# Score units in one slot less of each pair, and one gate portion ahead of its first transposes

## The chip, the cores and the metric

One core of a Trainium2 chip runs the whole kernel. The metric is the device time of one execution in microseconds (us); lower is better. Matmuls and transposes run on TensorE (PE), elementwise work on VectorE (DVE) and ScalarE (ACT), some helpers on GpSimd (POOL), and transfers are issued by SyncE (SP) and POOL.

## The reference

A decoder block on 1024 tokens of width 1024. What bears on the change is the attention part: 8 query heads (two per pair of heads, four heads per key group), three attention branches per head, and a gate per branch.

```python
s = einsum(q, k_cmp) * scale;  p_cmp = masked_softmax(s, pos_c <= t)        # 63 compressed keys
s_sel = einsum(qb, k_sel) * scale;  p_sel = masked_softmax(s_sel, kpos <= qpos)  # causal, all blocks
s_win = einsum(qb, k_win) * scale;  p_win = masked_softmax(s_win, wmask)    # window of 512
o = g[0] * o_cmp + g[1] * o_sel + g[2] * o_win
x = x + (sigmoid(ga) * (o @ w_branch_attn) + sigmoid(gb) * b) @ w_out       # ga, gb: columns of h @ w_in
```

## The kernel before

The stages are: input projections, a pooling branch, the attention stage, the output projections, and an MLP. The attention stage lies between about 336 and 694 us of the trace, and the change touches it alone.

**Pairs.** The stage walks over 32 pairs (L718): query tile i from 0 to 7, and in each the four head pairs hp from 0 to 3. For a pair there is a part A and a part B. Iteration n of the loop at L736 writes part A of pair n between the steps of part B of pair n-1.

**Part A** (`units_a`, L662) is four score units, in this order: selected keys of head 0 (`unit_sel`), window of head 0 (`unit_win`), selected keys of head 1, window of head 1. A unit writes its scores with PE into a tile `psS` (L578, L579), adds masks with PE (L584), takes the row maximum on DVE (L595) and the exponential on ACT (L596). From pair 12 on there are two `psS` tiles, so a unit needs the tile of the unit two before it. The fourth unit also ends the pair's softmax: it makes the factors `cc` (L650 to L652), scales the rows `pS` on DVE (L657, L658) and `pW` on ACT (L659). Odd hp add a fifth entry, `nxt`, which splits the next 512 columns of queries (`split_q`, L564 to L571).

**Part B** (`units_b`, L670) has a list of steps. A slot transposes one group of probability blocks into `psT` on PE (`tr`, L686) and splits it into `ph` on ACT (L689) and `pl` on DVE (L690). The products with the values (`pv`, L697) follow one slot later and have no slot of their own. A last slot without a transposition ends the list. So `nslot` is the number of groups plus one: 3, 4, 5, 6, 7, 7, 8, 8 for the pairs of i = 0 to 7.

**Where the units go.** At slot k the loop writes entries of part A until their count reaches ceil(k * na / nslot), with na = 4, or 5 for odd hp; then `finish_units` writes the masks and the softmax; then comes the slot's transposition.

**Gate portions.** `ga_terms` (L546) holds 128 portions of three matmuls each into `psG`, which compute the merge gate `ga`, in eight blocks of 16; the weights of the last block are loaded only after an earlier pair's output is written (`after=`, L550). `advance` (L723) writes as many portions as the part B done so far has earned: 20 at first, and then in proportion to the pairs' weights. In the kernel before it is called after the transposition of every slot.

The text of the loop is a list in order of rank and not yet the order on the engines. The tile layer draws up each engine's order when the kernel is built, from this rank and from what it reckons to be ready, so a piece of later rank can stand in front.

Of the kernel before, what the change touches and what calls it, by code (L numbers as in the profile page):

```python
# [49 lines left out]
def build(tc, a, out, dbg=None):  # L50
# [13 lines left out]
    def pool(stack, name, bufs=1, space=None, side=None):  # L64
        kw = dict(name=name, bufs=bufs, reuse_waits="tile")
        if space is DRAM:
            kw.pop("reuse_waits")
        if space is not None:
            kw["space"] = space
        if side is not None:  # L70
            kw["side"] = side
        return stack.enter_context(tc.tile_pool(**kw))
# [362 lines left out]
    def load_q(i, g):  # L435
        qi = qp.tile([P, HALF], F32, name="qi", bufs=2)
        nc.sync.dma_start(qi, qd[i][:, g * HALF:(g + 1) * HALF])
        return qi
# [93 lines left out]
    with ExitStack() as st:  # L532
# [31 lines left out]
        def split_q(qi):  # L564
            ps = psT.tile([P, HALF], F32, name="psT").rearrange("p (h n) -> p h n", h=4)
            for h in range(4):
                nc.tensor.transpose(ps[:, h], qi[:, h * P:(h + 1) * P], ident)
            qh = wk.tile([P, 4, P], F32R, name="qh", bufs=2)
            ql = wk.tile([P, 4, P], F32R, name="ql", bufs=2)
            nc.scalar.copy(qh, ps)  # L570
            nc.vector.tensor_tensor(ql, ps, f(qh), op=SUB)  # L571
            return qh, ql
# [9 lines left out]
        def finish_units():  # L582
            for ps, m, last, joint in masks_due:
                nc.tensor.matmul(ps, lhsT=identb, rhs=m, start=False, stop=last, skip_group_check=joint)  # L584
            for fn in softmax_due:
                fn()
            masks_due.clear()
            softmax_due.clear()
# [73 lines left out]
        def units_a(i, hp, q):  # L662
            w0 = max(0, i - WT)
            u = dict(i=i, hp=hp, g=hp // 2, w0=w0, nw=(i + 1 - w0) * P, pS=[], pW=[],
                     q=[(q[0][:, 2 * (hp % 2) + e], q[1][:, 2 * (hp % 2) + e]) for e in range(2)])
            for n in ("nm", "sm", "cc"):
                u[n] = wk.tile([P, 2, 3], F32, name=n, bufs=3)
            return u, [lambda e=e, fn=fn: fn(u, e) for e in range(2) for fn in (unit_sel, unit_win)]
# [54 lines left out]
        def advance(w):  # L723
            nonlocal done, given, ending
            done += w
            if len(bseq) and n >= len(pairs) - 1:
                ending += 0.4 * LAST / nslot
            while given < nterm and given < FIRST + (nterm - FIRST - LAST) * done / total + ending:
                next(fill, None)
                given += 1  # L730
# [4 lines left out]
        bseq, bw = [], 0  # L735
        for n in range(len(pairs) + 1):  # L736
            aseq = []
            if n < len(pairs):
                i, hp = pairs[n]
                if n == 12:  # L740
                    sctx.close()
                    psS = pool(sctx, "psS2", bufs=2, space=PSUM)
                u, aseq = units_a(i, hp, q)
                if hp % 2:
                    def nxt(j=2 * i + hp // 2 + 1):
                        nonlocal q, qnext
                        if j < 2 * NT:
                            q = split_q(qnext)
                            if j + 1 < 2 * NT:
                                qnext = load_q((j + 1) // 2, (j + 1) % 2)  # L750
                    aseq.append(nxt)
            na, nslot = len(aseq), max(1, sum(o for _, o in bseq))
            ia = k = 0
            for fn, slot in bseq or [(None, True)]:
                if slot:
                    k += 1
                    while ia < na and ia * nslot < k * na:
                        aseq[ia]()
                        ia += 1
                    finish_units()  # L760
                if fn is not None:
                    fn()
                if slot:
                    advance(bw / nslot)
            assert ia == na
            if n >= 2 and len(wsum) < 32 and summed < 27 * done / total:
                i, hp = pairs[n - 2]
                made[:] = [oT[0:1, hp, i * P:i * P + 4]]
                next(sums, None)
                summed += 1  # L770
            if n < len(pairs):
                bseq, bw = units_b(u), weight[n]
# [317 lines left out]
```

## Time and profile before

| | us |
|---|---|
| median of 3 runs (1469.38 to 1476.09) | 1470.88 |
| profiled execution, its own time | 1470.37 |
| its span | 1468.3 |
| PE busy | 1424.3 (97%) |
| DVE busy | 1008.9 (69%) |
| ACT busy | 756.4 (52%) |

The profile gives one execution. The span is from its first to its last instruction, 2.1 us less than the execution's time. A row of a timeline has the start in us, the duration in us, the engine, the line of the kernel, the operation, the tile written and the tiles read, the size, how many equal instructions it stands for, and in brackets the idle time of the engine just ahead of it with what ended it.

### The profile page before, as it was taken

To read this page: it belongs to the slowest core of one execution; us is meant where nothing else is said; L and a number is where in the kernel's file an instruction comes from. 1 tells how busy PE (TensorE), PEld (TensorE's weight loads), DVE (VectorE), ACT (ScalarE), POOL (GpSimd) and SP (SyncE) were. 2 spreads that over 40 slices of the span, in tenths; PEclk is the share of its full clock that TensorE was granted. 3 is DMA by queue.
4 is the path that set the end of the run, shared out by engine and by line. 5 is a ranking of instruction groups with operands and counts; after the bars stand their busy time and mean duration, and the time that the engine had idled before them with its cause. 6 is when DMAs were issued, how large, how long until landed. Compare 5 with 4: busy or idle time off the path is not lost.

```text
span 1468.3 us, 20380 instructions
## 1 busy us (share of the span) xinstructions
PE 1424.3 (97%) x7187; PEld 1177.9 (80%) x7187; DVE 1008.9 (69%) x1953; ACT 756.4 (52%) x1551; POOL 144.8 (10%) x207
## 2 busy tenths in 40 slices
PE   9989999999999999988999999999999999999996
PEld 7877888887778888776888888888888888888885
DVE  4793551114888888886758567667897386669996
ACT  4553231124888877776435363674344454764451
POOL 0006433222111211100000000000000000000000
PEclk9999999999999999999999999999999999999998
DMA  8334388886877777732845533333333223333323
GB/s 312 91 113 135 107 203 205 200 213 164 189 191 180 183 193 188 185 79 72 257 146 178 154 92 98 95 95 99 93 96 99 94 93 95 101 99 94 96 84 115
DMA packets 129109, 204.62 MB, mean 139 GB/s; under 512 B 9840, under 2 KB 60784, under 8 KB 128496
## 3 DMA queue, kind: packets, MB, share of 16 engines
q1 hardware_dynamic: 110800, 135.96, 29.9%
q0 software_dynamic: 17920, 67.11, 20.0%
q8 instruction: 56, 0.92, 0.2%
q14 instruction: 45, 0.37, 0.1%
q10 hardware_dynamic: 288, 0.27, 0.1%
HBM read 186.52 MB, written 83.89 MB: 184 GB/s over the span
## 4 chain that ended last, share of the span: by engine, by line
PE 89%; DVE 6%; ACT 3%; DMA 1%; issue 1%; SPq 0%; DVEq 0%; ACTq 0%
PE psm L78 17%; PE psm L77 17%; PE psm L79 17%; PE psF L78 5%; PE psF L79 5%; PE psF L77 5%; PE oacc L697 5%; PE psT L686 4%; PE psS L578 2%; PE psG L77 2%; PE psS L579 2%; PE psG L78 2%; PE psG L79 2%; PE acc L77 1%; PE acc L78 1%; PE acc L79 1%
## 5 line engine op out<-in xcount | busy, mean ns | idle before, releaser
L77 PE MATMUL psm<-mv,whi 128*128 128x512 f32 x896 | 350.6, 391 | 0.0
L78 PE MATMUL psm<-mv,whi 128*128 128x512 f32 x896 | 350.6, 391 | 0.0
L79 PE MATMUL psm<-mv,wlo 128*128 128x512 f32 x896 | 350.4, 391 | 0.0
L906 ACT CAST whi<-wraw 128x512 fp32r<-128x512 f32 x224 | 138.9, 620 | 257.3 <-PE psm L78 192.6
L82 DVE TENSOR_TENSOR wlo<-wraw,whi 128x512 fp32r<-128x512 f32 x289 | 197.8, 688 | 89.7 <-ACT whi L906 69.9
L78 PEld LDWEIGHTS psm<-mv,whi 128*128 128x128 f32 x896 | 168.3, 188 | 36.8
L77 PEld LDWEIGHTS psm<-mv,whi 128*128 128x128 f32 x896 | 168.3, 188 | 36.7
L79 PEld LDWEIGHTS psm<-mv,wlo 128*128 128x128 f32 x896 | 168.3, 188 | 36.7
L181 ACT CAST whi<-wraw 128x512 fp32r<-128x512 f32 x113 | 69.8, 621 | 125.4 <-PE psF L78 59.2
L690 DVE TENSOR_TENSOR pl<-psT,ph 128x512 fp32r<-128x512 f32 (+1 forms) x160 | 102.3, 648 | 31.3 <-ACT ph L689 29.6
L689 ACT CAST ph<-psT 128x512 fp32r<-128x512 f32 (+1 forms) x160 | 87.7, 556 | 47.9 <-PE psT L686 47.1
L595 DVE TENSOR_REDUCE nm<-psS 128x1 f32<-128x64 f32 (+8 forms) x192 | 100.2, 540 | 15.4 <-PE psS L584 10.1
L82 POOL TENSOR_TENSOR wlo<-wraw,whi 128x512 fp32r<-128x512 f32 x48 | 68.0, 1469 | 90.4 <-ACT whi L181 60.0
L77 PE MATMUL psF<-xh,whi 128*128 128x512 f32 x192 | 74.8, 390 | 0.0
L79 PE MATMUL psF<-xh,wlo 128*128 128x512 f32 x192 | 74.8, 390 | 0.0
L78 PE MATMUL psF<-xl,whi 128*128 128x512 f32 x192 | 74.7, 389 | 0.0
L596 ACT ACTIVATE pS<-psS,nm 128x64 f32<-128x64 f32 (+8 forms) x128 | 68.1, 534 | 8.7 <-DVE nm L595 8.0
L697 PE MATMUL oacc<-ph,vst 128*128 128x256 f32 x264 | 63.8, 320 | 4.1 <-ACT ph L689 2.7
L886 ACT CAST mv<-mt 128x512 fp32r<-128x512 f32 x96 | 59.0, 617 | 16.3 <-DVE mt L884 11.8
L82 DVE TENSOR_TENSOR mv<-mt,mv 128x512 fp32r<-128x512 f32 x96 | 65.1, 685 | 1.1 <-ACT mv L886 0.6
L686 PE MATMUL psT<-cf,pS 128*128 128x128 f32 x352 | 60.5, 277 | 4.5 <-DVE pS L657 4.2
L697 PE MATMUL oacc<-pl,vst 128*128 128x256 f32 x264 | 57.1, 295 | 3.1 <-DVE pl L690 3.0
(257 smaller groups left out, 2850.8 us busy)
## 6 DMA issues: line engine op xcount, KB each, us to landing
wraw<-wsw_ff SPq DMA_DIRECT2D x128, 256.0 KB
wraw<-in_w_ff SPq DMA_DIRECT2D x96, 256.0 KB
wsw_ff<-in_w_ff POOLq DMA_DIRECT2D x16, 1024.0 KB, 9.0
wsw_ff<-wsw_ff POOLq DMA_DIRECT2D x16, 1024.0 KB, 9.2
wraw<-in_w_in SPq DMA_DIRECT2D x48, 256.0 KB
wraw<-in_w_out SPq DMA_DIRECT2D x32, 256.0 KB
xt<-in_x SPq DMA_DIRECT2D x8, 512.0 KB
qd<-q SPq DMA_DIRECT2D x16, 256.0 KB
```

What stands on the lines that cost most here:

```text
L77: nc.tensor.matmul(ps, lhsT=sh, rhs=mh, start=first and i == 0, stop=False, skip_group_check=more)
L78: nc.tensor.matmul(ps, lhsT=sh, rhs=ml, start=False, stop=False, skip_group_check=more)
L79: nc.tensor.matmul(ps, lhsT=sl, rhs=mh, start=False, stop=last and i == n - 1, skip_group_check=more)
L82: eng.tensor_tensor(lo, src, f(hi), op=SUB)
L181: nc.scalar.copy(h, v)
L595: nc.vector.tensor_reduce(nm, v, axis=AX.X if flat else AX.XY, op=MAX, negate=True)
L596: nc.scalar.activation(p if flat else p.rearrange("p (a n) -> p a n", a=2), v, AF.Exp, bias=nm, accum_out=sm)
L686: nc.tensor.transpose(ps[:, j, e], src[e][:, c0:c0 + P], ident)
L689: nc.scalar.copy(ph[:, :n], ps[:, :n])
L690: nc.vector.tensor_tensor(pl[:, :n], ps[:, :n], f(ph[:, :n]), op=SUB)
L697: nc.tensor.matmul(o, lhsT=v, rhs=part[:, j], start=gi == 0 and j == 0 and part is ph, stop=2 * gi + j == nb - 1 and part is pl)
L906: nc.scalar.copy(hi, raw)
```

## The change

The entries of part A are spread over `nslot - 1` slots and not over `nslot`: at slot k their count reaches ceil(k * na / (nslot - 1)), so that all of them stand ahead of the last transposition. And in the first slot of a pair `advance` is called ahead of the transposition, in place of behind it. The number of portions that each call earns stays the same.

```diff
                 if slot:
                     k += 1
-                    while ia < na and ia * nslot < k * na:
+
+                    while ia < na and ia * max(1, nslot - 1) < k * na:
                         aseq[ia]()
                         ia += 1
                     finish_units()
+                    if k == 1:
+                        advance(bw / nslot)
                 if fn is not None:
                     fn()
-                if slot:
+                if slot and k > 1:
                     advance(bw / nslot)
```

## Rows read from the trace of the kernel before

**Rows 1.** The page: busy time of each engine.

```profile
PE 1424.3 (97%) x7187; PEld 1177.9 (80%) x7187; DVE 1008.9 (69%) x1953; ACT 756.4 (52%) x1551; POOL 144.8 (10%) x207
```

**Rows 2.** Busy time of each engine in the attention stage, by stretches.

```profile
core 0: us, PE busy (x) PEld busy (x) DVE busy (x) ACT busy (x) POOL busy (x), PEclk, DMA share, GB/s
336.00:430.00 94.00, 86.73 (x549) 69.97 (x549) 71.39 (x225) 68.74 (x228) 18.28 (x19) 1.00 0.72 171
430.00:606.00 176.00, 175.38 (x1217) 149.19 (x1216) 147.73 (x322) 138.66 (x330) 28.76 (x33) 1.00 0.78 194
606.00:673.00 67.00, 56.70 (x398) 46.50 (x398) 56.02 (x108) 50.93 (x110) 6.58 (x7) 1.00 0.44 99
673.00:694.00 21.00, 20.88 (x128) 17.56 (x126) 12.37 (x27) 10.28 (x21) 0.37 (x1) 1.00 0.20 63
```

**Rows 3.** The same stretches, instructions of the gate tile psG alone (PE, PEld, DVE).

```profile
336.00:430.00 94.00, 40.85 (x144) 25.31 (x144) 3.80 (x6) 1.00 0.72 171
430.00:606.00 176.00, 58.65 (x186) 31.13 (x186) 5.12 (x8) 1.00 0.78 194
606.00:673.00 67.00, 1.63 (x6) 1.05 (x6) 0.68 (x1) 1.00 0.44 99
```

**Rows 4.** Waits of PE, 606 to 673 us: total us, times, longest us.

```profile
PE psS L578 <- ACT pS L596: 2.7, 3, 1.3
PE oacc L697 <- ACT ph L689: 2.0, 4, 1.0
```

**Rows 5.** Timeline of PE in that stretch: five of the rows with a wait.

```profile
619.60 0.50 PE L578 MATMUL psS<-kds,qh 128*128 128x512 f32 x1 [1.42 <-ACT qh L570]
...
635.60 0.50 PE L578 MATMUL psS<-kds,qh 128*128 128x512 f32 x1 [0.75 <-ACT pS L596]
...
637.71 0.88 PE L686 MATMUL psT<-cf,pS 128*128 128x128 f32 x6 [0.39 <-DVE pS L657]
...
639.66 0.50 PE L697 MATMUL oacc<-pl,vst 128*128 128x256 f32 x2 [0.22 <-DVE pl L690]
...
663.86 0.50 PE L578 MATMUL psS<-kds,qh 128*128 128x512 f32 x1 [1.34 <-ACT pS L596]
```

**Rows 6.** Timeline of DVE between pair 28's last score unit and its first transposes.

```profile
630.84 0.82 DVE L595 TENSOR_REDUCE nm<-psS 128x1 f32<-128x640 f32 x1 [0.15 <-PE psS L584]
...
633.09 1.23 DVE L595 TENSOR_REDUCE nm<-psS 128x1 f32<-128x1024 f32 x1 [0.24 <-PE psS L584]
634.23 0.16 DVE L650 TENSOR_SCALAR cc<-sm 128x6 f32<-128x6 f32 x1
...
636.09 0.74 DVE L657 TENSOR_SCALAR pS<-pS,cc 128x1024 f32<-128x1024 f32 x1
```

**Rows 7.** Timeline of PE: one slot with no score unit and no gate.

```profile
640.00 0.60 PE L686 MATMUL psT<-cf,pS 128*128 128x128 f32 x4
...
640.91 0.60 PE L686 MATMUL psT<-cf,pS 128*128 128x128 f32 x4
```

**Rows 8.** Timeline of PE ahead of pair 18's first transposes.

```profile
504.62 0.47 PE L77 MATMUL psG<-xh,whi 128*128 128x512 f32 x1
...
506.97 0.40 PE L77 MATMUL psG<-xh,whi 128*128 128x512 f32 x1
...
507.66 0.40 PE L77 MATMUL psG<-xh,whi 128*128 128x512 f32 x1
...
508.05 0.44 PE L686 MATMUL psT<-cf,pS 128*128 128x128 f32 x2
```

**Rows 9.** Waits of PE, 336 to 430 us.

```profile
PE psT L686 <- DVE pS L657: 2.9, 4, 0.8
PE oacc L697 <- DVE pl L690: 1.4, 2, 1.1
```

**Rows 10.** Two early stretches, all engines: PE idle, then running.

```profile
82.00:84.00 2.00, 0.00 (x0) 0.00 (x0) 2.00 (x9) 0.44 (x3) 0.45 (x1) 0.50 0.58 186
84.00:86.00 2.00, 1.84 (x9) 1.87 (x10) 1.64 (x5) 0.29 (x2) 0.00 (x0) 0.50 0.46 146
```

## The prediction

> **What bounds the kernel now.** I read the page's busy times first. PE is busy for 1424.3 of 1468.3 us [rows 1], so the kernel is bound by TensorE, and an edit that neither removes nor adds a matmul can only give back what PE stands idle, 44 us in the whole span. The next view is the busy time by stretches of the attention stage, the only stage that the change touches [rows 2]. There PE is idle for 94 - 86.73 = 7.3 us up to 430, for 0.6 us from 430 to 606, for 67 - 56.70 = 10.3 us from 606 to 673 and for 0.1 us after it: 18.3 us in all. That is the ceiling of any gain. The other two engines are no bound, but near one: DVE has 147.73 of 176 us in the middle stretch (0.84).
>
> Why is the middle full and the stretch behind it not? The same stretches for the gate tile alone tell it [rows 3]. A portion is three matmuls, so the rows hold 144/3 = 48 portions up to 430, 186/3 = 62 up to 606, and 6/3 = 2 from there to 673. The gate matmuls fill PE's gaps while they last; then the gaps show. They run ahead of the text: by line 728 some 20 + 92 x 214/296 = 86 portions are earned when pair 25 ends at about 606 (214 and 296 are sums of line 719's weights), and 110 have run. So the order on PE is not the order of the text, and a gate portion fills wherever PE would otherwise wait.
>
> What PE waits for in the bare stretch is in the list of waits [rows 4] and in the timeline [rows 5]. They gather at a pair's boundary: the next pair's score units wait for a `psS` tile that ACT still reads (0.75 and 1.34 us), the first transposes wait for the scaled rows `pS` (0.39), the first products for `pl` (0.22), and once the new queries for `qh` (1.42). DVE's timeline shows the chain behind it at pair 28 [rows 6]: the reduce of the last unit starts at 630.84, the factors at 634.23, the scaling at 636.09, and the rest of the first transposes run at 637.71 [rows 5]. That is 6.9 us, with a reduce of the next pair (1.23 us at 633.09) in between.
>
> **Part one: units one slot less.** The positions follow from the ceiling rule. With 8 slots and 4 entries the units go from slots 1, 3, 5, 7 to 1, 2, 4, 6; with 7 slots from 1, 2, 4, 6 to 1, 2, 4, 5. With 8 slots and 5 entries (odd hp) they go from 1, 2, 4, 5 and `nxt` in 7 to 1, 2, 3, 5 and `nxt` in 6: there the last unit stays where it was. Going through all n, the last unit comes one slot earlier for n = 14, 16 and 17 to 24 (middle stretch), for 26, 28 and 30 (bare stretch), and in most early pairs. No instruction is added or removed. What is gained is lead: a slot without units and gates takes PE 640.91 - 640.00 = 0.91 us [rows 7].
>
> *Term 1, boundaries in the bare stretch.* Pairs 28 and 30 wait at least 0.75 + 0.39 + 0.22 and 1.34 us [rows 5]; 0.91 us of lead each can take off 1.8. The next pair's units stand in PE's order ahead of the transposes and wait for their own tile, so not all of it arrives. I take -1.3 (ends -1.8 and 0).
>
> *Term 2, the queries.* For n = 27 and 29 `nxt` moves from slot 7 to 6, ahead of one more transposition. The 1.42 us wait for `qh` [rows 5] is one of them: ACT reached that copy late. I take -0.6 (ends -0.9 and 0; its DMA, the next `load_q`, is one and is needed eight slots later).
>
> *Term 3, the middle.* There PE waits for nothing, so a shorter chain does not show at once. At pair 18, gates run from 504.62 until the first transposes at 508.05, a portion each 507.66 - 506.97 = 0.69 us [rows 8]. With 0.91 us less to cover, each of the ten boundaries there (n = 14, 16, 17 to 24) needs 1.3 portions less, the pairs advance faster, and up to 9.1 us of portions are left for the bare stretch, which after terms 1 and 2 still has 10.3 - 1.9 = 8.4 us idle. The ends are 0 (the portions run ahead just the same) and -8.4. Two things cut it: the units already float in front of their place, so I let half of the lead survive (4.6 us), and DVE's 147.73 us pressed into ten microseconds less would be 0.89 of the time; and three quarters of what is left should land in a wait. I take -3.4.
>
> *Term 4, the early pairs.* Up to 430 the first transposes wait four times, 2.9 us, and products twice, 1.4 us [rows 9]. Of these four boundaries one is odd and unmoved. I take -0.8 (ends -2.2 and 0).
>
> *Term 5, crowding.* Units 1 and 2 now stand in neighbouring slots and, in odd pairs of 8 slots, unit 3 two slots behind unit 1. What queues behind a unit's reduce on DVE is that slot's `pl` (for which the products wait) and behind its exponential on ACT the slot's `ph`. The nearest rows are the small waits for `ph`, 2.0 us in four [rows 4]. I take +1.0 (ends 0 and +8.9, the second rival).
>
> **Part two: a portion ahead of the first transposes.** It adds nothing and moves at most one portion (0.69 us) by one transposition in rank. As the portions run some 24 ahead of the text, this rank decides nothing while any are left, and in the bare stretch there are none. I take 0. If the rank did decide, a portion could fill one of the four early waits (-2.0 at the best, three of 0.69), or hold up transposes that are ready (0.69 us each, hidden as long as `ph` and `pl` are not awaited). The loads of the portions keep their order on SP, the weight sums on POOL keep theirs, and no wait is added to either queue.
>
> The sum is -1.3 - 0.6 - 3.4 - 0.8 + 1.0 = -5.1 us. Against the profiled execution of 1470.4 that is 1465.3; the median of the runs stands 0.5 above that execution, so the forecast is 1465.8 us, with 1461 to 1470 as its own range.
>
> **A rule on the clock.** The bare stretch has 10.3 us of small gaps, and the granted clock is 1.00 (2.4 GHz) throughout [rows 2]; it is 0.50 (1.2 GHz) in 84 to 86 us, behind a stretch of 2 us in which PE ran nothing [rows 10]. The Trainium skill ("TensorE: Matmul & The Clock Gate", section "A second HAM failure mode: psum-queue depth-cycling") says that small pauses between groups of matmuls, while a kernel cycles through PSUM buffers, can make the clock swing between its levels. By that rule, which speaks against moving units onto each other's two tiles, the stretch's 56.70 us of PE work would take up to twice as long, some 1520 us in all. The trace does not agree so far, as such pauses left the clock at 1.00; I give it one chance in a hundred.
>
> **Rivals.** *All gaps are covered (faster).* If the whole lead of ten boundaries is kept, 9.1 us of portions (13) remain for the bare stretch, which with terms 1 and 2 is more than its idle time; with the early waits -10.3 - 0.8 = -11, or 1460. For it speaks that where portions exist only 0.6 of 176 us are idle [rows 2]; against it, that DVE would be near 0.9 and that the text's order is not PE's order.
>
> *Crowding (slower).* A unit needs the tile of the unit two before. At pair 29 the tile whose reduce began at 633.09 [rows 6] came free for PE only at 635.60 [rows 5], 2.5 us later, and before that it had to be filled. Two bare slots are 1.8 us plus the unit between. In eight odd pairs (n = 17 to 31) one such distance falls from three slots to two. With the longest wait of that kind, 1.34 us [rows 5], in each: the four late ones cost 5.4 us openly; the four in the middle use up 5.4/0.69 = 8 portions, which at 176/62 = 2.8 us a portion bares 22 us more of the stage, and at 10.3/67 that costs 3.5. Together +8.9, or 1479. It decides once the tile is held longer than two slots with their unit. Against it: in 7-slot pairs units already stand in slots 1, 2 and 3, and the middle has no such wait.
>
> *Nothing happens.* The order is drawn up by readiness, units already run ahead of their slot as the `psS` tiles allow, and the rank does not reach PE: 1470.5.
>
> **How the numbers follow.** The forecast has 0.52, covered gaps 0.20, nothing 0.14, crowding 0.13, the clock 0.01. A measurement of this kernel can tell about 0.5% (7.4 us) from no change, so faster means below 1463.5 and slower above 1478.2. Faster gets nearly all of the covered gaps (0.19) and the lower part of the forecast (0.12): 0.31. Slower gets two thirds of crowding and the clock: 0.10. The rest, 0.59, is no change that can be told. The range of 1458.5 to 1475 takes in the covered gaps with the early waits and leaves out most of crowding.
>
> **What would show it.** Right: more than 15 gate matmuls between the end of pair 25 and 673, fewer than 62 portions in the middle with the pairs there ending earlier, less than 5.5 us of PE idle in the bare stretch, no 1.42 us wait for `qh`, and the early stretch little changed. Term 3 is wrong if the portions again run out at pair 25. Crowding would show as more waits of `psS` on ACT. Part two is wrong at nothing if the first transposes of early pairs wait less with a portion right ahead of them. Wrong altogether: a change outside 336 to 694 us, or a stage that shrinks with PE's idle time unchanged.

## The result

The changed kernel takes 1464.15 us in the median of 6 runs (1462.67 to 1464.90), the kernel before 1472.2 us beside it; the ratio is 0.9949, with a 95% interval of 0.9937 to 0.9961. Forecast were 1465.8 us and a range of 1458.5 to 1475. The profiled execution took 1463.95 us, 6.4 less than the one of before.

The page of the kernel after, its span and the busy time of each engine, answers to [rows 1]:

```profile
span 1462.0 us, 20421 instructions
PE 1424.5 (97%) x7187; PEld 1180.2 (81%) x7187; DVE 1007.2 (69%) x1953; ACT 756.8 (52%) x1551; POOL 144.3 (10%) x207
```

PE has the same work to 0.2 us and the span is 6.3 us shorter: what went is idle time of PE. The stretches of [rows 2] for the kernel after, all engines:

```profile
336.00:430.00 94.00, 86.54 (x546) 69.14 (x545) 72.15 (x225) 69.29 (x228) 16.30 (x17) 1.00 0.70 170
430.00:606.00 176.00, 173.00 (x1200) 147.10 (x1200) 150.87 (x330) 142.13 (x335) 29.70 (x34) 0.99 0.78 191
606.00:673.00 67.00, 65.95 (x461) 56.16 (x459) 57.36 (x112) 52.40 (x115) 6.14 (x6) 1.00 0.50 115
```

and those of [rows 3], the gate tile alone:

```profile
336.00:430.00 94.00, 40.71 (x140) 24.74 (x140) 3.43 (x5) 1.00 0.70 170
430.00:606.00 176.00, 50.33 (x159) 26.83 (x159) 4.79 (x7) 0.99 0.78 191
606.00:673.00 67.00, 17.05 (x53) 8.83 (x52) 1.37 (x2) 1.00 0.50 115
```

The stretch that was bare, 606 to 673 us, has 1.05 us of PE idle time in place of 10.3. It now holds 53/3 = 18 gate portions where two were, and the middle has 53 in place of 62. Of the waits of PE there, [rows 4] and [rows 5], two are left in the kernel after, and none for `psS` or `qh`:

```profile
PE oacc L697 <- ACT ph L689: 0.3, 1, 0.3
PE oacc L697 <- DVE pl L690: 0.3, 1, 0.3
```

Fixed stretches cut pairs at different points, so the further comparison goes by pairs: from the stage's first gate matmul to the copy that ends pair 10, to the one that ends pair 25, and to the one that ends pair 31. Before:

```profile
336.30:430.19 93.89, 86.91 (x550) 70.11 (x550) 71.34 (x224) 68.47 (x228) 18.47 (x19) 1.00 0.72 171
430.19:606.15 175.96, 175.34 (x1217) 149.18 (x1217) 147.66 (x323) 138.63 (x329) 28.57 (x33) 1.00 0.78 193
606.15:691.87 85.72, 75.41 (x514) 62.59 (x513) 67.63 (x130) 60.60 (x129) 6.95 (x7) 1.00 0.38 90
```

After:

```profile
336.95:430.90 93.95, 87.33 (x552) 70.00 (x553) 71.84 (x224) 68.35 (x228) 15.35 (x16) 1.00 0.70 171
430.90:604.92 174.02, 171.02 (x1188) 145.40 (x1186) 149.45 (x326) 141.07 (x334) 29.00 (x34) 0.99 0.78 192
604.92:685.25 80.33, 79.13 (x541) 67.47 (x540) 65.02 (x126) 58.41 (x125) 6.85 (x7) 1.00 0.42 99
```

The stage is 355.57 us long before and 348.30 after, 7.3 less. PE's idle time in the three groups of pairs goes from 7.0, 0.6 and 10.3 us to 6.6, 3.0 and 1.2 us, in sum from 17.9 to 10.8, 7.1 less. The stage began 0.65 us later in this execution and 0.3 us were lost behind it, which makes the 6.3 us of the span. The gate tile alone in the last six pairs, before and after:

```profile
606.15:691.87 85.72, 13.25 (x46) 7.95 (x47) 1.36 (x2) 1.00 0.38 90
604.92:685.25 80.33, 25.55 (x81) 13.43 (x80) 2.05 (x3) 1.00 0.42 99
```

That is 46/3 = 15 portions before and 81/3 = 27 after. So the gain shows in the last six pairs, and the middle pays 2.4 us of idle time for it.

At pair 28 the kernel after shows the cover at work. DVE's chain of [rows 6], in the kernel after:

```profile
626.29 0.82 DVE L595 TENSOR_REDUCE nm<-psS 128x1 f32<-128x640 f32 x1
...
628.88 0.17 DVE L650 TENSOR_SCALAR cc<-sm 128x6 f32<-128x6 f32 x1
...
630.57 0.74 DVE L657 TENSOR_SCALAR pS<-pS,cc 128x1024 f32<-128x1024 f32 x1
```

and PE beside it:

```profile
630.21 0.47 PE L78 MATMUL psG<-xl,whi 128*128 128x512 f32 x1
...
631.45 0.40 PE L77 MATMUL psG<-xh,whi 128*128 128x512 f32 x1
631.69 0.38 PE L686 MATMUL psT<-cf,pS 128*128 128x128 f32 x2
...
632.37 0.82 PE L686 MATMUL psT<-cf,pS 128*128 128x128 f32 x6
```

From the last unit's reduce to the transposes it takes 632.37 - 626.29 = 6.1 us where it took 6.9 [rows 5, 6], and in the part in which PE stood idle, it runs gate matmuls.

### The profile page after: what moved, and what is told of

It is laid out like the page before. It is cut to its first block, busy times and chain, and to the rows that moved or that the text cites. A ratio compares the mean times of both kernels' runs of the same rounds, so it can differ in the third digit from the quotient of the medians.

```text
span 1462.0 us, 20421 instructions
## 1 busy us (share of the span) xinstructions
PE 1424.5 (97%) x7187; PEld 1180.2 (81%) x7187; DVE 1007.2 (69%) x1953; ACT 756.8 (52%) x1551; POOL 144.3 (10%) x207
## 4 chain that ended last, share of the span: by engine, by line
PE 89%; DVE 6%; ACT 3%; DMA 1%; issue 1%; SPq 0%; DVEq 0%; ACTq 0%
PE psm L79 17%; PE psm L78 17%; PE psm L77 17%; PE oacc L697 5%; PE psF L78 5%; PE psF L79 5%; PE psF L77 5%; PE psT L686 4%; PE psS L578 2%; PE psS L579 2%; PE psG L77 2%; PE psG L78 2%; PE psG L79 2%; PE acc L77 1%; PE acc L78 1%; PE acc L79 1%
## 5 line engine op out<-in xcount | busy, mean ns | idle before, releaser
L595 DVE TENSOR_REDUCE nm<-psS 128x1 f32<-128x64 f32 (+8 forms) x192 | 99.1, 540 | 15.8 <-PE psS L584 10.3
```

The source lines that it names most:

```text
L595: nc.vector.tensor_reduce(nm, v, axis=AX.X if flat else AX.XY, op=MAX, negate=True)
```

## The experiments

All runs were compared with the kernel before on the same chip. The table gives, for the profiled execution of each, PE's idle time in pairs 0 to 10, 11 to 25 and 26 to 31, and the gate portions in the last six pairs, each from the two views shown above. These are single executions, and the granted clock moves them: in e3 and e4, whose early pairs are as in the kernel before, the 5.8 and 5.9 us there in place of 7.0 go with a stretch at a lower clock (shown at the end), in which PE is busy longer (88.1 us in place of 86.9) and waits less.

| run | ratio (95% interval) | idle, us | portions in the last pairs |
|---|---|---|---|
| before | 1 | 7.0, 0.6, 10.3 | 15 |
| after | 0.9949 (0.9937 to 0.9961) | 6.6, 3.0, 1.2 | 27 |
| e1_units_only | 0.9957 (0.9943 to 0.9970) | 6.9, 3.1, 1.2 | 27 |
| e2_gates_only | 0.9995 (0.9986 to 1.0004) | 7.3, 0.7, 9.9 | 15 |
| e3_units_mid | 0.9980 (0.9970 to 0.9990) | 5.8, 1.6, 7.9 | 19 |
| e4_units_late | 1.0005 (0.9997 to 1.0014) | 5.9, 0.7, 10.2 | 13 |
| e5_units_early | 1.0024 (1.0014 to 1.0033) | 7.0, 5.3, 4.5 | 23 |
| e8_units_upto24 | 0.9974 (0.9962 to 0.9985) | 6.9, 3.2, 2.0 | 28 |
| e6_two_less | 0.9964 (0.9951 to 0.9977) | 5.2, 2.1, 4.0 | 27 |
| e7_first16 | 0.9971 (0.9960 to 0.9983) | 6.6, 2.0, 5.8 | 24 |
| e12_two_less_early | 0.9919 (0.9904 to 0.9934) | 8.0, 2.8, 0.5 | 31 |
| e11_hold_block6 | 1.0068 (1.0051 to 1.0084) | 6.7, 7.9, 9.2 | 29 |
| e9_spend_early | 1.0289 (1.0269 to 1.0308) | 8.1, 24.2, 10.8 | 14 |
| e10_spend_early_before | 1.0342 (1.0327 to 1.0358) | 8.4, 27.0, 9.3 | 14 |

**Each part alone.** The units' part alone:

```diff
-                    while ia < na and ia * nslot < k * na:
+                    while ia < na and ia * max(1, nslot - 1) < k * na:
```

> Only the first part: the entries spread over one slot less, advance called behind the transposition as before. Theory (the units' lead is everything): the whole gain, ratio 0.994 to 0.996, and PE idle in 606 to 673 us about 1 us as with the whole change. Rival (the portion ahead of the first transposes covers the boundary waits): less than half of the gain, ratio above 0.997.

The portion ahead of the first transposes alone:

```diff
                     finish_units()
+                    if k == 1:
+                        advance(bw / nslot)
...
-                if slot:
+                if slot and k > 1:
```

> Only the second part: the first slot's portions ahead of the transposition, the units where they were. Theory (rank decides nothing while portions run ahead): no difference, ratio 0.999 to 1.001, bare stretch of 606 to 673 us with about 10 us of PE idle as before. Rival (portions in front cover the boundaries): at least half of the gain, ratio 0.997 or less.

The first gives 0.9957, whose interval holds the ratio of the whole change, with the same idle times and portions; the second gives 0.9995, with an interval that holds 1. In the second kernel the order of PE's instructions in the stage differs from the kernel before only between 677.5 and 681.3 us, in and after the first transposes of pair 31. Part two does nothing.

**The lead in one group of iterations only.** The same line with `nslot - less`, where `less` is 1 in the named iterations and 0 elsewhere:

```diff
-                    while ia < na and ia * nslot < k * na:
+                    less = 1 if 13 <= n < 25 else 0   # e3; e4: n >= 25; e5: n < 13; e8: n < 25
+                    while ia < na and ia * max(1, nslot - less) < k * na:
```

> The units' lead only in iterations 13 to 24, whose boundaries lie in the middle stretch where PE has no wait. Theory (lead there saves gate portions, which fill the bare stretch): most of the gain though no wait stood where the edit is, ratio 0.995 to 0.997, fewer than 56 portions from 430 to 606 us and PE idle in 606 to 673 us under 5 us. Rival (the gain is made at the boundaries of the bare stretch themselves): ratio 0.999 to 1.001 and idle of about 10 us in the bare stretch.

> The units' lead only from iteration 25 on, whose boundaries lie in the bare stretch. Theory (portions left over from the middle): a small part of the gain, 1 to 2.5 us, ratio 0.998 to 0.9995, two portions in the stretch as before and still 7 to 9 us of PE idle. Rival (the lead shortens the waits on the spot): most of the gain, 5 us or more, ratio 0.9965 or less, with idle in the stretch down to 5 us without any more portions.

> The units' lead only up to iteration 12, whose boundaries lie before 430 us and where the whole change left PE's idle time as it was (7 us). Theory A (the early lead saves gate portions although it saves no wait; they reach the bare stretch): half of the gain, ratio 0.997 to 0.9985, three or more portions in the last six pairs beyond those of before and their PE idle time clearly under 10 us. Theory B (the gain comes from the middle's lead alone, and its missing half from middle and late together): ratio 0.9995 to 1.001 and 10 us of idle in the last pairs.

> The units' lead up to iteration 24, early and middle, and none in the last seven. Theory A (the lead at the last boundaries is worth nothing by itself, portions kept are everything): the whole gain, ratio 0.9945 to 0.9965, and under 3 us of PE idle in the last six pairs. Theory B (portions and a late lead are needed together): about the gain of the middle alone, ratio 0.9975 to 0.9985, and over 6 us of idle there.

In the middle alone the lead gives 0.9980: less than expected, but where no wait stood. 58 portions run there in place of 62, the last pairs have 19 in place of 15, and their idle time falls by 2.4 us.

In the last iterations alone, where the waits were, it gives nothing. Four waits in PE's timeline of that run:

```profile
621.76 0.51 PE L697 MATMUL oacc<-ph,vst 128*128 128x256 f32 x2 [1.48 <-ACT ph L689]
...
637.38 0.50 PE L578 MATMUL psS<-kds,qh 128*128 128x512 f32 x1 [1.41 <-ACT pS L596]
...
641.62 0.51 PE L697 MATMUL oacc<-pl,vst 128*128 128x256 f32 x2 [1.12 <-DVE pl L690]
...
665.36 0.49 PE L578 MATMUL psS<-kds,qh 128*128 128x512 f32 x1 [1.29 <-ACT pS L596]
```

The 1.42 us wait for `qh` [rows 5] is gone, and a product waits 1.48 us for `ph` instead; at the boundary of pair 28 the wait for the tile is 1.41 us where it was 0.75, and 1.12 us are spent on `pl`. Each wait that was taken away has come back as another.

In the early iterations alone the lead makes the kernel slower, 1.0024, which neither theory had. It saves 1.3 portions there (46.7 in place of 48); in the middle 55 run in place of 62, but with 5.3 us of waits where 0.6 were, so the waits have moved forward. That is not what makes it slower: in sum PE's idle time is 16.8 us, 1.1 less than in the kernel before. The stage of this profile is 3.0 us longer (358.58) because PE's busy time is 4.1 us longer, and the last pairs have a granted clock of 0.96:

```profile
606.89:693.73 86.84, 82.32 (x538) 69.38 (x537) 68.32 (x131) 61.20 (x130) 6.64 (x7) 0.96 0.39 92
```

0.04 of 82.32 us is 3.3 us of work at full clock. This execution is the fastest of the twelve, 2.4 us below their median; what slows the others is not shown.

The three separate effects add up to -0.20 + 0.05 + 0.24 = +0.09%, and together they make -0.43%. They don't add. With the early and the middle lead together it is -0.26%, with 28 portions and 2.0 us of idle time in the last pairs: theory A in the idle time, close to theory B in the ratio. Whether the late lead, worth nothing where PE has no portions to run, brings the rest once it has is not shown: the intervals of e8 and e1 overlap.

**Taking the cover away.** The portions are given a rank far ahead, in the whole change and in the kernel before:

```diff
-        LAG, FIRST, LAST = 1, 20, 16
+        LAG, FIRST, LAST = 1, 96, 16
```

> The whole change, but the portions are given a rank far ahead (96 in place of 20 earned at once), so that they are spent before the last pairs. The leads are all there, the cover is not. Theory (the gain is cover, portions kept for the last pairs): the gain is gone and more, ratio 1.000 to 1.004, with 10 us or more of PE idle in the last six pairs. Rival (the gain is shorter boundaries, whatever covers them): ratio 0.994 to 0.997 as with the whole change.

> The units as before the change, with the portions given the rank that spends them before the last pairs (96 earned at once). Partner of the run with the whole change and the same rank (1.029). Theory (a unit's lead is worth something only as long as portions are there to be saved): as slow, ratio 1.027 to 1.031, and 0.13 to 0.15 us of PE idle per us from the middle on, as there. Rival (the lead shortens the boundaries by itself): slower than that run by 5 us or more, ratio 1.032 or above.

All 112 portions that can run early have run by the end of pair 10, and from there on PE waits. The middle and last pairs with the change's units:

```profile
480.25:649.46 169.21, 145.02 (x1032) 119.88 (x1030) 144.56 (x319) 134.45 (x321) 21.65 (x28) 1.00 0.75 184
649.46:734.09 84.63, 73.83 (x501) 62.54 (x500) 64.74 (x124) 57.55 (x123) 5.61 (x6) 0.98 0.37 89
```

and with the units of before:

```profile
480.00:656.70 176.70, 149.67 (x1021) 123.65 (x1022) 143.02 (x312) 131.79 (x316) 21.89 (x27) 0.97 0.72 176
656.70:743.47 86.77, 77.52 (x513) 63.41 (x513) 68.16 (x131) 60.24 (x128) 6.95 (x7) 0.98 0.36 87
```

Without cover PE is idle 24.2 + 10.8 = 35.0 us in 253.8 (0.138 per us) with the lead, and 27.0 + 9.3 = 36.3 in 263.5 (0.138) without it. In idle time the lead of 0.91 us [rows 7] shortens a boundary of the 15 middle pairs by (27.0 - 24.2)/15 = 0.2 us, and those of the last pairs not at all. The times differ by 8.7 us all the same, 1513.8 against 1522.45: the size that the rival named. In the two profiles the 21 pairs differ by 9.6 us, of which 1.3 are idle time and the rest is PE's busy time, 145.0 + 73.8 against 149.7 + 77.5 us for the same matmuls; the granted clock in the middle is 1.00 against 0.97. The clock explains some 4.7 us (below). The other 4.9 us, 0.23 us a pair in these two executions, go with the lead without any cover, so the theory that it is worth nothing there is not borne out. That the clock is not all of it shows over the runs too: one of the four with the lead had a mean granted clock of 0.987, as all four without it, and took 1514.47 us where these took 1521.53 or more.

The lost cover costs more than the idle time that it uncovers. With the lead the stage is 40.5 us longer than in the kernel before (396.04 against 355.57): 25.2 of them are idle time and 15.3 are busy time of PE (353.0 against 337.7), of which the clock explains 2.9. PE's records break off 119 times in that stage, and 48 times in the kernel before. Four transpositions in a row take 0.60 us [rows 7], and one by itself 0.27, so (0.60 - 0.27)/3 = 0.11 us is what one adds in a row; by this estimate each break counts 0.27 - 0.11 = 0.16 us as busy that a full engine would not spend, 11 us for 71 breaks more, most of the 12.4 left.

The expectation for the first of the two, 1.000 to 1.004, was far too small: it counted the last six pairs and not the 15 of the middle that lose their cover too.

**Keeping portions by a wait.** The last but one block's weights wait for an earlier pair's output too:

```diff
-                              after=oT[0:1, hp, i * P:i * P + 4] if m == NK - 1 else None)
+                              after=oT[0:1, hp, i * P:i * P + 4] if m >= NK - 2 else None)
```

> The units as before, but the weights of the last but one block of portions wait for an earlier pair's output too, so that 32 portions, not 16, are left for the last pairs. Theory (kept portions help only where the middle needs fewer): the waits move from the last pairs into the middle, ratio 0.998 to 1.003, PE idle of the stage 15 us or more. Rival (the middle wastes its portions, keeping them is all): idle in the last pairs under 4 us without more in the middle, ratio 0.994 to 0.997.

It is slower, 1.0068, more than either expectation had, with 23.7 us of idle time in the stage: the bare stretch moved, and no portion ran from 560 to 640 us. To the waits came one of 2.3 us for the late weights themselves (`psG` on `whi`). How the middle does with portions that are held back and still spread was not tried.

**A later rank for the portions, without the lead.** 16 portions earned at once in place of 20, the units as before:

```diff
-        LAG, FIRST, LAST = 1, 20, 16
+        LAG, FIRST, LAST = 1, 16, 16
```

> The units as before, with 16 portions in place of 20 earned at once: a new draw of the engines' order without any lead for the units. Theory (the order's luck is small): ratio 0.999 to 1.001, idle of the stage 17 to 19 us. Rival (any redraw moves the time as much as this change did): ratio off by 0.003 or more, either way.

0.9971, without any lead, is over half of the change's gain: idle time 14.4 us in the stage, 24 portions in the last pairs. The theory (0.999 to 1.001) fails, and the rival's 0.003 is all but reached. But the edit is not a redraw alone. It lowers the rank of the portions too, by four at the start, and so holds cover back; the gate tile in the first and the last group of pairs:

```profile
335.45:425.00 89.55, 36.10 (x126) 22.27 (x127) 3.42 (x5) 1.00 0.70 170
601.55:687.04 85.49, 20.75 (x71) 12.18 (x72) 2.05 (x3) 1.00 0.40 93
```

Up to pair 10 run 126/3 = 42 portions in place of 48, and 24 are left for the last pairs in place of 15. So 3.9 us can be had without any lead, with fewer portions spent early. How much of it is the later rank and how much the chance of another order stays open: no run draws another order with units and portions ranked as before, and in e2 the order hardly changes. Whether single effects of 0.2% in the table (e3, e5, e8) come from the lead itself or from where the new order happens to put portions cannot be told. What all runs have in common is the relation of the last two columns. Leaving out the runs that move the bare stretch itself (e9 to e11), each step from 13 and 15 portions (10 us idle) over 19 (7.9), 23 and 24 (4.5, 5.8) to 27 and more (4.0 to 0.5) takes the waits of the last pairs away: from the kernel before to the change (10.3 - 1.2)/(27.0 - 15.3) = 0.8 us a portion, near the 0.69 us that a portion runs [rows 8].

**More of it.** Two slots less everywhere, and two less only up to iteration 12:

```diff
-                    while ia < na and ia * nslot < k * na:
+                    less = 2   # e12: 2 if n < 13 else 1
+                    while ia < na and ia * max(1, nslot - less) < k * na:
```

> The entries spread over two slots less in place of one; the portions where they were. Doubles the lead and presses the units closer onto the two score tiles. Theory (lead saves portions, two tiles are held some 2.5 us): about half as much again or no more gain, ratio 0.993 to 0.996, with waits of psS on ACT up to 3 us in the stage. Rival (crowding decides already at two slots less): slower than before, ratio 1.002 to 1.006, with over 6 us of waits for psS.

> The entries spread over two slots less up to iteration 12 (where the run with two less everywhere ended its pairs 6 us sooner with 6 portions fewer) and over one less from there; the portions where they were. Theory (portions saved early are kept for the last pairs): as fast as the whole change or up to 3 us faster, ratio 0.992 to 0.995, PE idle of the stage under 11 us. Rival (the savings only move waits from one stretch to another): ratio 0.996 to 0.999 and idle of 12 us or more.

Two less everywhere is no better than one (0.9964), and PE's waits for `psS` stay at 2.0 us in the stage, where the rival had over 6. Two less in the early pairs and one from there on gives 0.9919, the best of all: its interval lies below that of the change. The median is 1459.67 us. By pairs, all engines:

```profile
335.41:426.86 91.45, 83.44 (x533) 67.92 (x534) 70.67 (x223) 66.95 (x226) 13.93 (x15) 1.00 0.67 162
426.86:600.23 173.37, 170.57 (x1193) 145.06 (x1191) 150.12 (x327) 140.58 (x334) 29.53 (x34) 1.00 0.79 196
600.23:681.35 81.12, 80.64 (x552) 69.07 (x551) 65.28 (x127) 59.06 (x127) 7.05 (x7) 1.00 0.42 101
```

31 portions are left for the last pairs, and 0.5 us of idle time. The stage is 345.94 us long, 2.4 less than the change's. Its idle time, 11.3 us, is near the change's 10.8; PE's busy time is 334.65 in place of 337.48, and of these 2.8 us the change's one drop of the clock (below), which this run's middle does not have, is 1.7. The interval of the whole says that it is faster than the change; what share of that is the clock's and what the portions' was not separated.

## Why the prediction held, step by step

**What bounds it** was read right: PE's work stayed the same, and the gain is 7.1 us of PE's idle time in the one stage. That the middle was full because portions run ahead, and the last pairs bare because they had run out, is what e9 and e10 show: without portions the middle waits 0.14 and 0.15 us per us, the last pairs of the kernel before 0.12. Idle time was not quite the ceiling that it was taken for, as the busy time can fall too: it is 3.0 us less in e12 (334.65) than in the kernel before.

**Terms 1 and 2** (the boundaries of the bare stretch and `qh`, -1.3 and -0.6) failed as they were priced. The lead in these iterations alone gave 1.0005. The step that failed is that a wait was taken for a price that its removal pays: the next wait behind it took its place, as e4's rows show.

**Term 3** (the middle's lead, -3.4) came out at 0.9980, -2.9 us, through the way that was forecast: fewer portions in the middle, more in the last pairs. Its inner working is not borne out. Half of 0.91 us was to be saved at each of ten boundaries; without cover it is 0.2 us a pair, and the whole change saves 7.1/31 = 0.23 us a pair over all boundaries. So the lead of one boundary was priced too high, and as e7 shows, a later rank of the portions does as much as e3 without any lead; that the lead itself left the portions over in e3 is argued and not shown. For it speaks that every run with the lead in the middle gains while the cover is there (e1, e3, e6, e8, e12), and the two with the lead elsewhere alone (e4, e5) do not.

**Term 4** (early pairs, -0.8) has the wrong sign alone (+0.24%, with less idle time and a lower clock in the profile), and in the whole change the early idle time went from 7.0 to 6.6 us. What it leaves for later is little at one slot less, 46.7 portions run by pair 10 in place of 48, and more at two (40.3 in e6 and e12).

**Term 5** (crowding, +1.0) was too small, the waits of the middle grew by 2.4 us; but of these only 0.4 us are for `psS`, and for `pl` and `ph`, which the term named, 1.9; how much of it is crowding and how much the thinner cover was not separated. The rival *crowding* did not come true at one slot less, nor at two.

**Part two** was right at nothing (e2). **The rival of covered gaps** came true in the last pairs, 1.2 us idle, and not in the early ones. The sum was -5.1 where the profiles differ by 6.4: two terms too much, one in the wrong place, and the effect of all together, which no term had, in their stead. That the sum lies so near is in part luck.

## What to carry to other kernels

Where an engine is full because independent work fills its gaps, look for where that work ends: a wait saved in the full part is paid out there, and a wait removed in the bare part is likely to be replaced by the next one. Keep such filler for the stretch that has none, by its rank (e7) and not by a wait (e11), and count how much is left when it starts; here each portion of 0.69 us that was kept took about 0.8 us of waits away. When a layer below redraws the order of the engines, run another order beside the edit that leaves edit and filler as they were (none was run here) before an effect of 0.2 or 0.3% is put down to a mechanism.

## What the hardware showed

The granted clock dropped in places where I had not expected it. In the kernel after, PE waits 0.72 and 0.51 us at 483 us, and the next stretches, all engines, show:

```profile
482.00:486.00 4.00, 2.77 (x14) 2.21 (x13) 3.04 (x7) 3.53 (x10) 1.05 (x2) 0.77 0.96 158
486.00:490.00 4.00, 4.00 (x29) 3.85 (x28) 2.88 (x5) 2.48 (x5) 0.74 (x1) 0.80 1.29 371
```

That cost about 4 x 0.23 + 4 x 0.20 = 1.7 us of work at full clock, in a place where the kernel before kept 1.00. In the kernel with the units of before and the portions spent, the same view around a wait of 2.04 us at 581 has the lower level, 1.2 GHz, for a whole stretch:

```profile
578.00:582.00 4.00, 1.76 (x10) 1.07 (x10) 3.87 (x12) 3.51 (x8) 1.75 (x2) 0.83 0.25 38
582.00:586.00 4.00, 4.00 (x17) 3.71 (x18) 1.99 (x5) 1.79 (x6) 0.00 (x0) 0.50 1.12 201
586.00:590.00 4.00, 4.00 (x29) 3.73 (x27) 1.92 (x4) 2.30 (x7) 0.00 (x0) 0.82 0.79 291
```

There 17 matmuls and transposes fill a stretch that 29 fill in the next one, at 0.82. In that profile the clock is below 1.00 in four places of the stage, in its partner in two. In stretches of 4 us, busy time times the missing share of the clock sums to 7.6 us up to 743 us in the one and to 2.9 us up to 734 in the other. This is 4.7 of the 8.1 us by which PE's busy time in the stage differs (361.1 against 353.0). PE's records break off 131 times in the one and 119 times in the other; by the estimate of 0.16 us a break that is 1.9 of the other 3.4. The Trainium skill ("TensorE: Matmul & The Clock Gate", section "A second HAM failure mode: psum-queue depth-cycling") says that small pauses between groups of matmuls, while a kernel cycles through PSUM buffers, can make the clock swing. The prediction gave that one chance in a hundred as a loss over the whole bare stretch, which did not come; as single drops that cost 2 us or so it is in these traces, and not in the stage of this profile of the kernel before, whose bare stretch had 10.3 us of such pauses at 1.00.

The order of the instructions does not settle it. Up to 455 us PE's order in e3, e4 and e11 is that of the kernel before, instruction by instruction, and all three profiles have a drop at about 410 us that the profile before has not. The kernel before, and e4:

```profile
410.00:414.00 4.00, 4.00 (x27) 3.32 (x25) 3.12 (x8) 2.90 (x7) 1.03 (x1) 1.00 0.56 108
410.00:414.00 4.00, 4.00 (x19) 3.69 (x18) 2.90 (x9) 2.75 (x9) 1.03 (x1) 0.58 0.33 77
```

So a single profile at 1.00 does not say that a stretch is free of drops. Why one wait brings a drop and a longer one does not stays open.
